# Layer norm and final norm with a token to a partition: sums, roots and reciprocals on two columns, brought back along the tokens by products with the identity

## The chip, the cores and the metric

The kernel runs on one core of a Trainium2 chip. TensorE (PE in the profile; its weight loads are PEld) multiplies matrices into PSUM; VectorE (DVE), ScalarE (ACT) and GpSimd (POOL) work on elements; SyncE (SP) issues most transfers. The metric is the device time of one execution in microseconds (us).

## The reference, cut to what matters

The program is an encoder trunk over 256 tokens with 2048 channels: a convolution module, a feed-forward layer, a gated DeltaNet, a second feed-forward layer, and a final norm. The change touches the middle of the convolution module and the final norm:

```python
u = a * jax.nn.sigmoid(gate)
u = depthwise_conv_centred(u, w_dw) + b_dw
u = jax.nn.silu(layernorm(u, ln_g, ln_b))      # mean and variance over the 2048 channels
return u @ w_pw2 + b_pw2
...
return rmsnorm(h, final_norm)                  # x * rsqrt(mean(x*x) + eps) * w
```

## The kernel before, in words

Activations lie with the channels along the 128 partitions and the 256 tokens along the free dimension, so that 2048 channels are 16 tiles of 128x256. A sum over channels is therefore a sum over partitions and over tiles. The kernel forms it on TensorE: a 128x128 matrix of ones as the stationary operand times a tile, accumulated over the tiles (line 341 in the layer norm, line 286 in the other norms). The result is a 128x256 tile whose every partition holds the same 256 sums, so the root and the reciprocal that follow run over 256 elements in each partition, and every tile can be multiplied by them at once.

Weights arrive in f32 and are split into a rounded half (`hi`, a cast on ScalarE, line 181) and the rest (`lo`, a subtraction on VectorE, line 182). A product of a weight block with an activation tile is then two or three fast matmuls. Sums of the norms are plain f32 products; in the trace each such product shows as two weight loads and two matmuls.

**The convolution loop** (`conv_module`, `for j in range(KD)`) makes one tile per turn: two 2048-deep products (lines 211 to 213), the gate, and the 31 taps of the depthwise convolution spread over TensorE (line 387), ScalarE with GpSimd (395, 396) and VectorE (404). `second(j)` then adds the tile's sum (`s1`) and, after a square on ScalarE (line 351), the sum of squares (`s2`) with `add`. The first four tiles give a rough mean (`shift`), which is taken off, so that the variance may be formed from sums.

**The layer norm** follows the last tile. In the last turn the conv chain has the priority `LAST`; five weight tiles of the next product are prepared ahead (`highs`, line 414, on ScalarE; `weights`, line 422, on VectorE). Then, in an order written out by hand for VectorE and ScalarE (`manual_schedule`): mean `dm` (465), its square `dq` (466, ScalarE), `var` (467), root `rt` (469), a small operation that loads the table of Silu (`warm`, 292), `weights(2)`, reciprocal `lr` (472), `ml` (473), and then for each tile `mul` (474), `sub` (479), Silu (480), cast (481), `low` (484). TensorE has 26 products without a use (`FILL`, line 456) after the last sum, and then the products of the next weight `pw2`, five output tiles at a time (lines 206, 207, 209).

**The final norm** (`finish`): ScalarE scales the 16 tiles of `h` (1061); the sum of squares comes as `ss` (15 tiles, summed on GpSimd) and `rest` (the last tile's square, line 275); `token_sum` (286), root (297), reciprocal `own` into PSUM (301), a copy `rstd` into SBUF by ScalarE (1067); VectorE multiplies 12 tiles by `own` (1073), GpSimd four by `rstd` (1071: tiles 1, 5, 9, 13), and each tile is stored (1074) from ScalarE's queue where its number is even, and from SP's where it is odd.

The order of the instructions in each queue is set when the program is built, by a planner that simulates the time of each instruction and takes the ready one with the highest priority; `high_priority(n)` raises it. `with tc.issue_after(x)` makes every instruction in the block that runs on the engine of `x` come behind `x` in that engine's queue; those on other engines are free. PSUM has eight banks, which the tags share: three `lin`, two `b`, one each of `sum`, `a` and `g`.

Of the kernel before, what the change touches and what calls it, by code (L numbers as in the profile page):

```python
# [26 lines left out]
PSB = {"lin": 3, "sum": 1, "a": 1, "b": 2, "g": 1}  # L27
HP = 550
OUT0 = 26
LAST = 2500  # L30
# [6 lines left out]
FIRST = 4  # L37
# [8 lines left out]
XB = 7  # L46
FIRSTS = 5
PRE = 5
FILL = 26
MORE = 2  # L50


# [25 lines left out]
def fv(ap, off, *dims):  # L78

    return bass.AP(ap.tensor, ap.offset + off, [list(ap.ap[0]), *[list(d) for d in dims]])  # L80


class Trunk:
# [199 lines left out]
    def token_sum(self, *ts):  # L283
# [2 lines left out]
            self.nc.tensor.matmul(acc, self.mat("ones"), t, start=(n == 0), stop=(n == len(ts) - 1))  # L286
        return acc

    def warm(self, func, after):

        t = self.sp.tile([P, 1], F32, tag="warm", bufs=1, name=self.nm("warm"))
        self.nc.scalar.activation(t, after[:, :1], func)
# [18 lines left out]
    def conv_module(self, next_norm):  # L311
        nc, tc, sp = self.nc, self.tc, self.sp
        self.new_h()
        self.load_first([self.pw1[0], self.pw1[KD]])
        with tc.tile_pool(name="conv", bufs=1, reuse_waits="tile") as cv:
# [6 lines left out]
            new = lambda tag, bufs: cv.tile([P, S], F32, tag=tag, bufs=bufs, name=self.nm(tag))  # L322
# [10 lines left out]
            shift = None  # L333
            sums = {}

            def add(key, t, n, last):

                if n == 0:
                    tag = "a" if key == "s1" else "sum"
                    sums[key] = self.ps.tile([P, S], F32, tag=tag, bufs=PSB[tag], name=self.nm(key))  # L340
                self.summed = nc.tensor.matmul(sums[key], self.mat("ones"), t, start=(n == 0), stop=last)

            def second(j):

                d = us[j]
                if j < SHIFTED:
                    nc.gpsimd.tensor_tensor(d, d, shift, op=ALU.subtract)
                if j >= FIRST:
                    add("s1", d, j - FIRST, j == KD - 1)
                sq = new("lsq", 2)  # L350
                self.sq_done = nc.scalar.activation(sq, d, AF.Square)
                add("s2", sq, j, j == KD - 1)
                ds.append(d)

            for j in range(KD):
# [4 lines left out]
                rstd = self.rstd  # L360
# [6 lines left out]
                with tc.high_priority(LAST if j == KD - 1 else 0):  # L367
# [6 lines left out]
                    acc = new(f"a{j}", 1)  # L374
                    npe, npool = NPE[j], NPOOL[j]
                    own = None
                    if j == KD - 1:
                        own = self.ps.tile([P, S], F32, tag="b", bufs=PSB["b"], name=self.nm("own"))
# [26 lines left out]
                    if own:  # L405
# [5 lines left out]
                        def highs(c):  # L411
                            r = raws[c][:, : CS * P]
                            hi, lo = (cv.tile([P, CS * P], F32R, tag=t, bufs=XB, name=self.nm(t)) for t in ("hi", "lo"))
                            nc.scalar.copy(hi, r)
                            pre[c] = (r, hi, lo)
                            return hi

                        def weights(c, after=None):

                            r, hi, lo = pre[c]  # L420
                            with tc.issue_after(after.ins) if after else nullcontext():
                                nc.vector.tensor_tensor(lo, r, hi.bitcast(F32), op=ALU.subtract)
                            pre[c] = [(hi[:, x * P : (x + 1) * P], lo[:, x * P : (x + 1) * P]) for x in range(CS)]

                        with tc.issue_after(scaled.ins):
                            self.warm(AF.Sqrt, tg)
                            for c in range(PRE):
                                pre_hi = highs(c)
                    if own:
# [5 lines left out]
                        t = nc.vector.tensor_tensor(acc, acc, part, op=ALU.add)  # L435
# [4 lines left out]
                            nc.vector.tensor_tensor(acc, acc, o, op=ALU.add)  # L440
                us.append(acc)
                if j < FIRST:
                    add("s1", acc, j, j == FIRST - 1)
                if j == FIRST - 1:
                    shift = new("shift", 1)
                    nc.scalar.activation(shift, sums["s1"], AF.Copy, scale=1.0 / (FIRST * P))
                    for i in range(FIRST):
                        second(i)
                elif j >= FIRST:
                    second(j)  # L450


            idle = self.ps.tile([P, 512], F32, tag="lin", bufs=PSB["lin"], name=self.nm("idle"))
            with tc.issue_after(self.summed.ins):
                for n in range(FILL):
                    nc.tensor.matmul(idle, pre_hi[:, :P], pre_hi, start=True, stop=True)

            dm, dq, var = new("dm", 1), new("dq", 1), new("var", 1)

            lr, ml = (self.ps.tile([P, S], F32, tag="b", bufs=PSB["b"], name=self.nm("ln")) for _ in range(2))  # L460
            order = range(KD)
            ys = [cv.tile([P, 2 * S], F32R, tag=f"y{j}", name=self.nm("y")) for j in order]

            with tc.high_priority(HP), tc.manual_schedule(engines={mybir.EngineType.DVE, mybir.EngineType.Activation}):
                nc.vector.tensor_scalar(dm, sums["s1"], 1.0 / D, None, op0=ALU.mult)
                nc.scalar.activation(dq, sums["s1"], AF.Square, scale=1.0 / D)
                known = nc.vector.scalar_tensor_tensor(var, sums["s2"], 1.0 / D, dq, op0=ALU.mult, op1=ALU.subtract)
                rt = self.sp.tile([P, S], F32, tag="rstd", bufs=2, name=self.nm("rstd"))
                nc.scalar.activation(rt, var, AF.Sqrt, scale=1.0, bias=self.c("eps5"))
                self.warm(AF.Silu, rt)  # L470
                weights(2)
                nc.vector.reciprocal(lr, rt)
                nc.vector.tensor_tensor(ml, dm, lr, op=ALU.mult)
                mul = lambda n: n < KD and nc.vector.tensor_tensor(ds[n], ds[n], lr, op=ALU.mult)

                def sub(n):

                    if n < KD:
                        self.begun = nc.vector.tensor_tensor(ds[n], ds[n], ml, op=ALU.subtract)
                        nc.scalar.activation(ds[n], ds[n], AF.Silu, scale=self.p("lng", n), bias=self.p("lnb", n))  # L480
                        nc.scalar.copy(ys[n][:, :S], ds[n])

                def low(n):
                    nc.vector.tensor_tensor(ys[n][:, S:], ds[n], ys[n][:, :S].bitcast(F32), op=ALU.subtract)

                mul(0)
                sub(0)
                mul(1)
                weights(3)
                sub(1)  # L490
                mul(2)
                for n in range(KD):
                    low(n)
                    if n == 1:
                        for c in range(4, PRE):
                            weights(c)
                    sub(n + 2)
                    mul(n + 3)
                    if n == 1:
                        begun = self.begun  # L500
            self.norm_begin()
            with tc.issue_after(begun.ins):
                self.ahead, self.split_ahead = [raws], pre[:PRE]
                first = self.products(self.pw2[:FIRSTS], KD, ys, wide=True, tags=("lin", "lin", "lin", "g", "a")[:FIRSTS], pool=cv, order=order)
            self.five = None
# [552 lines left out]
    def finish(self):  # L1058
        nc = self.nc
        for k in range(KD):  # L1060
            nc.scalar.activation(self.h[k], self.h[k], AF.Copy, scale=self.p("finn", k))

        own = self.ps.tile([P, S], F32, tag="b", bufs=PSB["b"], name=self.nm("own"))
        ss = [self.ss, self.rest]
        self.rsqrt(self.token_sum(*ss), 1.0 / D, self.c("eps6"), None, own)
        rstd = self.sp.tile([P, S], F32, tag="rstd", bufs=2, name=self.nm("rstd"))
        nc.scalar.copy(rstd, own)
        for k in range(KD):
            o = self.h[k]
            if k % 4 == 1:  # L1070
                nc.gpsimd.tensor_tensor(o, o, rstd, op=ALU.mult)
            else:
                nc.vector.tensor_tensor(o, o, own, op=ALU.mult)
            (nc.sync if k % 2 else nc.scalar).dma_start(self.out[:, k, :], o)
        self.free_h()
# [90 lines left out]
```

## Time and profile before

| | |
|---|---|
| runs | 2806.95, 2806.75, 2803.21 us; median 2806.75 |
| profiled execution | 2802.27 us, its span 2800.5 us |
| granted TensorE clock, mean | 0.998 |
| busy share | PE 98%, DVE 74%, ACT 63%, POOL 13% |
| convolution module up to the first product of `pw2` | 0 to 267.0 us of the span |
| last product of the program to the end | 2787.4 to 2800.5 us |

Times inside the profile count from the start of the span. A busy share is an average over stages; the two places that the change touches are two stretches of some 10 us, in which TensorE has little to do. Operations on one engine overlap at their ends, so that the start of the next can lie before the recorded end of the last.

### The profile page before, as it was taken

Reading aid. Unit: us, or ns where it says so; the run is one execution under the profiler, and the core shown is the slowest. Engines: PE = TensorE matmul, PEld = TensorE weight load, DVE = VectorE, ACT = ScalarE, POOL = GpSimd, SP = SyncE. Lnnn points to the kernel's source line nnn. Section 1 sums busy time; section 2 is a strip of 40 time slices with the busy share of each in tenths; the row PEclk is TensorE's granted clock in tenths of the full one; section 3 lists DMA queues with packets and bytes.
Section 4 is the critical chain, followed back from the end, with each engine's and each line's share of the span. In section 5 each row is a group of like instructions: output and inputs, shape, how many; then the busy total and the mean of one; then the engine's idle time right before and its main releaser. Section 6 shows DMA issues by size and latency. Waiting matters only on the chain.

```text
span 2800.5 us, 50212 instructions
## 1 busy us (share of the span) xinstructions
PE 2754.0 (98%) x18224; PEld 2510.1 (90%) x18224; DVE 2065.2 (74%) x3892; ACT 1759.7 (63%) x3716; POOL 367.9 (13%) x427
## 2 busy tenths in 40 slices
PE   8999999999999999999999999999999999999998
PEld 7998888888888889999999999998888888888887
DVE  8999876666666667889898989856666666665555
ACT  8877555555554445776978878765455555555443
POOL 3764310000000112000000000001110000000111
PEclk9999999999999999999999999999999999999999
DMA  5443565555556665776565665576666655566664
GB/s 188 137 146 127 179 202 189 189 189 190 191 188 194 198 199 176 237 235 201 174 231 168 227 197 193 182 254 189 190 209 190 191 189 188 189 189 187 189 191 139
DMA packets 170649, 532.88 MB, mean 190 GB/s; under 512 B 18944, under 2 KB 42752, under 8 KB 170400
## 3 DMA queue, kind: packets, MB, share of 16 engines
q1 hardware_dynamic: 169104, 528.37, 59.3%
q8 instruction: 143, 2.34, 0.3%
q10 hardware_dynamic: 1296, 1.30, 0.1%
q14 instruction: 106, 0.87, 0.1%
HBM read 500.69 MB, written 28.90 MB: 189 GB/s over the span
## 4 chain that ended last, share of the span: by engine, by line
PE 82%; ACT 6%; DVE 4%; DMA 4%; issue 2%; POOL 2%; SPq 0%; POOLq 0%; DVEq 0%; ACTq 0%
PE acc L207 39%; PE acc L206 20%; PE acc L213 5%; PE acc L212 5%; PE acc L211 5%; POOL a L396 2%; DVE lo L182 2%; PE psa L925 1%; PE psb L967 1%; ACT hi L181 1%; DMA raw<-in_win 1%; PE psb L990 1%; PE acc L209 1%; DMA raw<-in_wout 1%; PE psg L778 1%
## 5 line engine op out<-in xcount | busy, mean ns | idle before, releaser
L182 DVE TENSOR_TENSOR lo<-raw,hi 128x512 fp32r<-128x512 f32 x1759 | 1256.3, 718 | 641.6 <-ACT hi L181 634.3
L181 ACT CAST hi<-raw 128x512 fp32r<-128x512 f32 x1759 | 1076.3, 619 | 835.2 <-PE acc L207 658.4
L207 PE MATMUL acc<-xs,hi 128*128 128x512 f32 x2816 | 967.3, 392 | 0.0
L206 PE MATMUL acc<-xs,lo 128*128 128x256 f32 x2640 | 744.1, 282 | 0.0
L207 PEld LDWEIGHTS acc<-xs,hi 128*128 128x128 f32 x2816 | 517.0, 188 | 99.0
L211 PE MATMUL acc<-xs,hi 128*128 128x256 f32 x2064 | 585.7, 285 | 13.7 <-ACT hi L181 8.9
L213 PE MATMUL acc<-xs,lo 128*128 128x256 f32 x2064 | 586.5, 285 | 2.8 <-DVE lo L182 2.7
L212 PE MATMUL acc<-xs,hi 128*128 128x256 f32 x2064 | 585.0, 284 | 1.1 <-DVE xs L264 1.0
L206 PEld LDWEIGHTS acc<-xs,lo 128*128 128x128 f32 x2640 | 498.4, 189 | 8.4
L207 PE MATMUL acc<-hs,hi 128*128 128x512 f32 x1408 | 486.8, 391 | 0.0
L211 PEld LDWEIGHTS acc<-xs,hi 128*128 128x128 f32 x2064 | 389.6, 189 | 18.6 <-ACT hi L181 10.5
L213 PEld LDWEIGHTS acc<-xs,lo 128*128 128x128 f32 x2064 | 389.6, 189 | 11.9 <-issue 5.7
L212 PEld LDWEIGHTS acc<-xs,hi 128*128 128x128 f32 x2064 | 390.3, 189 | 6.6 <-issue 4.1
L206 PE MATMUL acc<-hs,lo 128*128 128x256 f32 x1376 | 388.3, 282 | 0.0
L207 PEld LDWEIGHTS acc<-hs,hi 128*128 128x128 f32 x1408 | 262.4, 188 | 52.8
L206 PEld LDWEIGHTS acc<-hs,lo 128*128 128x128 f32 x1376 | 260.1, 189 | 1.6
L532 POOL TENSOR_TENSOR tg<-tg,rstd 128x256 f32<-128x256 f32 x88 | 65.4, 744 | 905.6 <-ACT tg L531 905.6
L207 PE MATMUL acc<-ys,hi 128*128 128x512 f32 x512 | 177.7, 392 | 0.0
L396 POOL TENSOR_TENSOR a<-a,m 128x256 f32<-128x256 f32 x171 | 150.3, 880 | 97.3 <-ACT m L395 85.3
L206 PE MATMUL acc<-ys,lo 128*128 128x256 f32 x496 | 140.3, 284 | 2.2 <-DVE lo L182 2.2
L275 POOL TENSOR_TENSOR sq<-h 128x256 f32<-128x256 f32 x59 | 53.4, 905 | 543.4 <-DVE h L543 384.5
L711 DVE SCALAR_TENSOR_TENSOR u<-t,par_sb,u 128x254 f32<-128x254 f32 (+1 forms) x256 | 120.3, 480 | 2.3 <-ACT u L707 1.8
(239 smaller groups left out, 2910.1 us busy)
## 6 DMA issues: line engine op xcount, KB each, us to landing
raw<-in_gu SPq DMA_DIRECT2D x352, 512.0 KB, 4.5
raw<-in_win SPq DMA_DIRECT2D x194, 512.0 KB, 4.4
raw<-in_dn SPq DMA_DIRECT2D x160, 512.0 KB, 3.6
raw<-in_pw SPq DMA_DIRECT2D x94, 512.0 KB, 3.8
raw<-in_wout SPq DMA_DIRECT2D x64, 512.0 KB, 4.4
a_d<-am SPq DMA_DIRECT2D x32, 512.0 KB, 4.3
ar<-a_d SPq DMA_DIRECT2D x32, 512.0 KB, 5.0
raw<-in_dn SPq DMA_DIRECT2D x32, 256.0 KB, 3.6
```

What stands on the lines that cost most here:

```text
L181: nc.scalar.copy(hi, r)
L182: nc.vector.tensor_tensor(lo, r, hi.bitcast(F32), op=ALU.subtract)
L206: nc.tensor.matmul(acc[:, S:], lo, a[:, :S], start=False, stop=False)
L207: nc.tensor.matmul(acc, hi, a, start=first, stop=last)
L209: nc.tensor.matmul(acc[:, S:], lo, a[:, :S], start=False, stop=False)
L211: nc.tensor.matmul(acc[:, :S], hi, a[:, :S], start=first, stop=False)
L212: nc.tensor.matmul(acc[:, :S], hi, a[:, S:], start=False, stop=False)
L213: nc.tensor.matmul(acc[:, :S], lo, a[:, :S], start=False, stop=last)
L275: (nc.vector if last else nc.gpsimd).tensor_tensor(sq, h, h, op=ALU.mult)
L396: nc.gpsimd.tensor_tensor(acc, acc, m, op=ALU.add)
L532: nc.gpsimd.tensor_tensor(tg, tg, rstd, op=ALU.mult)
L711: nc.vector.scalar_tensor_tensor(u[:, lo:hi], t[:, lo + s : hi + s], w(i), u[:, lo:hi], op0=ALU.mult, op1=ALU.add)
```

## The change: what it does

The tile becomes the stationary operand, and a narrow constant the moving one. `sums["all"]` is one PSUM tile of 128x4: for each tile and each half `b` of the tokens, the 128x128 block of the tile is loaded as weights and multiplied by four columns of `sel`, of which one is all ones and three are zero. So the sums of 128 tokens land in one column, a token to a partition: columns 0 and 1 hold `s1`, 2 and 3 hold `s2`. The sums of the first four tiles, which give `shift`, stay as they were.

`dm`, `dq`, `var`, `rt`, `rc` and `mc` are then 128x2. `dq` moves from ScalarE to VectorE. `along` brings a column back: the column, read 128 times with a step of 0, is the stationary operand, the identity the moving one, and the product is a 128x128 block whose every partition holds the column's 128 values along the tokens. Two such products write `lr`, two write `ml`, both in PSUM as before. The 26 products without use become 6 behind the last sum and 10 behind `ml`.

Three orders change. The last tile's square gets the priority `LAST`. The products of `pw2` and the casts of their weights also stand behind that square (`issue_after(self.sq_done.ins)`). `weights(2)` comes after the reciprocal and `mc`.

In the final norm the squares' tiles are the stationary operand too, with one column of ones; each half of the tokens has its PSUM bank, its root (128x1) on ScalarE; one reciprocal of 128x2 follows. `along` is called twice: into `own`, which VectorE reads, and into `other`, which ScalarE copies to `rstd` for GpSimd.

```diff
-FILL = 26
+FILL = (6, 10)
...
+    def along(self, out, col):
+        for b in range(2):
+            t = self.nc.tensor.matmul(out[:, b * P : (b + 1) * P], fv(col, b, (0, P)), self.mat("ident"), start=True, stop=True)
+        return t
...
+                for b in range(2):
+                    self.summed = nc.tensor.matmul(sums["all"], t[:, b * P : (b + 1) * P], self.c("sel", 4 * (2 * key + b), 4),
+                                                   start=(n == 0 and b == 0), stop=(last and b == 1))
...
-                self.sq_done = nc.scalar.activation(sq, d, AF.Square)
-                add("s2", sq, j, j == KD - 1)
+                with tc.high_priority(LAST if j == KD - 1 else 0):
+                    self.sq_done = nc.scalar.activation(sq, d, AF.Square)
+                add(1, sq, j, j == KD - 1)
...
-                nc.vector.tensor_scalar(dm, sums["s1"], 1.0 / D, None, op0=ALU.mult)
-                nc.scalar.activation(dq, sums["s1"], AF.Square, scale=1.0 / D)
-                known = nc.vector.scalar_tensor_tensor(var, sums["s2"], 1.0 / D, dq, op0=ALU.mult, op1=ALU.subtract)
-                rt = self.sp.tile([P, S], F32, tag="rstd", bufs=2, name=self.nm("rstd"))
+                nc.vector.tensor_scalar(dm, s1, 1.0 / D, None, op0=ALU.mult)
+                nc.vector.tensor_tensor(dq, dm, dm, op=ALU.mult)
+                nc.vector.scalar_tensor_tensor(var, s2, 1.0 / D, dq, op0=ALU.mult, op1=ALU.subtract)
                 nc.scalar.activation(rt, var, AF.Sqrt, scale=1.0, bias=self.c("eps5"))
                 self.warm(AF.Silu, rt)
+                nc.vector.reciprocal(rc, rt)
+                nc.vector.tensor_tensor(mc, dm, rc, op=ALU.mult)
                 weights(2)
-                nc.vector.reciprocal(lr, rt)
-                nc.vector.tensor_tensor(ml, dm, lr, op=ALU.mult)
+                idles(FILL[0], self.summed)
+                self.along(lr, rc)
+                idles(FILL[1], self.along(ml, mc))
...
-            with tc.issue_after(begun.ins):
+            with tc.issue_after(begun.ins), tc.issue_after(self.sq_done.ins):
...
-        own = self.ps.tile([P, S], F32, tag="b", bufs=PSB["b"], name=self.nm("own"))
-        ss = [self.ss, self.rest]
-        self.rsqrt(self.token_sum(*ss), 1.0 / D, self.c("eps6"), None, own)
+        rt, rc = (self.sp.tile([P, 2], F32, tag=f"tail{n}", bufs=1, name=self.nm("rt")) for n in range(2))
+        sums = [self.ps.tile([P, 1], F32, tag=t, bufs=PSB[t], name=self.nm("tsum")) for t in ("sum", "a")]
+        for n, t in enumerate((self.ss, self.rest)):
+            for b in range(2):
+                nc.tensor.matmul(sums[b], t[:, b * P : (b + 1) * P], self.mat("ones")[:, :1], start=(n == 0), stop=(n == 1))
+        for b in range(2):
+            nc.scalar.activation(rt[:, b : b + 1], sums[b], AF.Sqrt, scale=1.0 / D, bias=self.c("eps6"))
+        nc.vector.reciprocal(rc, rt)
+
+        own, other = (self.ps.tile([P, S], F32, tag="b", bufs=PSB["b"], name=self.nm("own")) for _ in range(2))
+        self.along(own, rc)
+        self.along(other, rc)
         rstd = self.sp.tile([P, S], F32, tag="rstd", bufs=2, name=self.nm("rstd"))
-        nc.scalar.copy(rstd, own)
+        nc.scalar.copy(rstd, other)
```

More of the change, by code (lines that the diff above doesn't have):

```diff
@@ L336, in add @@
             def add(key, t, n, last):
[L338 to L341, printed above, removed]
+                if key == "first":
+                    if n == 0:
+                        sums[key] = self.ps.tile([P, S], F32, tag="a", bufs=PSB["a"], name=self.nm(key))
+                    nc.tensor.matmul(sums[key], self.mat("ones"), t, start=(n == 0), stop=last)
+                    return
+                if "all" not in sums:
+                    sums["all"] = self.ps.tile([P, 4], F32, tag="sum", bufs=PSB["sum"], name=self.nm("s"))
+                for b in range(2):
+                    self.summed = nc.tensor.matmul(sums["all"], t[:, b * P : (b + 1) * P], self.c("sel", 4 * (2 * key + b), 4),
+                                                   start=(n == 0 and b == 0), stop=(last and b == 1))
             def second(j):
@@ L348, in second @@
                 if j >= FIRST:
-                    add("s1", d, j - FIRST, j == KD - 1)
+                    add(0, d, j, False)
                 sq = new("lsq", 2)
-                self.sq_done = nc.scalar.activation(sq, d, AF.Square)
-                add("s2", sq, j, j == KD - 1)
+                with tc.high_priority(LAST if j == KD - 1 else 0):
+                    self.sq_done = nc.scalar.activation(sq, d, AF.Square)
+                add(1, sq, j, j == KD - 1)
                 ds.append(d)
@@ L442, in conv_module @@
                 if j < FIRST:
-                    add("s1", acc, j, j == FIRST - 1)
+                    add("first", acc, j, j == FIRST - 1)
                 if j == FIRST - 1:
                     shift = new("shift", 1)
-                    nc.scalar.activation(shift, sums["s1"], AF.Copy, scale=1.0 / (FIRST * P))
+                    nc.scalar.activation(shift, sums["first"], AF.Copy, scale=1.0 / (FIRST * P))
                     for i in range(FIRST):
@@ L453, in conv_module, with idles @@
             idle = self.ps.tile([P, 512], F32, tag="lin", bufs=PSB["lin"], name=self.nm("idle"))
[L454 to L458, printed above, removed]
+            def idles(n, after):
+                with tc.issue_after(after.ins):
+                    for _ in range(n):
+                        nc.tensor.matmul(idle, pre_hi[:, :P], pre_hi, start=True, stop=True)
+            dm, dq, var, rt, rc, mc = (cv.tile([P, 2], F32, name=self.nm("col")) for _ in range(6))
+            s1, s2 = sums["all"][:, :2], sums["all"][:, 2:]
             lr, ml = (self.ps.tile([P, S], F32, tag="b", bufs=PSB["b"], name=self.nm("ln")) for _ in range(2))
```

## Prediction

> **What bounds the kernel now.** I read the page's busy shares first, then the chain of waits around the layer norm and at the end, then timelines of single engines there, and the convolution loop by windows. The whole is bound by TensorE:
>
> ```profile
> PE 2754.0 (98%) x18224; PEld 2510.1 (90%) x18224; DVE 2065.2 (74%) x3892; ACT 1759.7 (63%) x3716; POOL 367.9 (13%) x427
> ```
>
> Time won elsewhere counts only where TensorE waits. It waits in the layer norm; in the chain of waits (start, length, what) the last 8 us before its first product at 267.00 are mostly other engines' work:
>
> ```profile
> 258.79 1.04 ACT hi L181 x2
> 259.82 0.33 ACT lsq L351
> ...
> 261.01 0.42 DVE var L467
> 261.44 0.60 DVE lo L422
> 262.04 1.75 DVE ln L472
> 263.81 0.43 DVE ln L473
> ...
> 267.00 0.50 PE acc L207
> ```
>
> Two weight casts stand ahead of the last square (line 351); a reciprocal over 256 elements takes 1.75; `lo` L422 (0.60) and `ml` (L473, 0.43) lie on the chain too. The other place is the end, all engines in order of time:
>
> ```profile
> 2788.86 0.51 ACT L1061 ACTIVATE h<-h,par_sb 128x256 f32<-128x256 f32 x1 [6.37 <-DVE sq L275]
> 2788.88 0.70 PE L286 MATMUL tsum<-sq,cst_sb 128*128 128x256 f32 x2 [1.50 <-DVE sq L275]
> 2789.62 0.47 ACT L297 ACTIVATE rstd<-tsum,cst_sb 128x256 f32<-128x256 f32 x1 [0.25 <-PE tsum L286]
> 2790.13 1.76 DVE L301 RECIPROCAL own<-rstd 128x256 f32<-128x256 f32 x1 [1.30 <-ACT rstd L297]
> 2791.92 0.37 ACT L1067 COPY rstd<-own 128x256 f32<-128x256 f32 x1 [1.83 <-DVE own L301]
> 2792.32 4.07 DVE L1073 TENSOR_TENSOR h<-h,own 128x256 f32<-128x256 f32 x12 [0.44 <-ACT rstd L1067]
> 2792.37 2.77 POOL L1071 TENSOR_TENSOR h<-h,rstd 128x256 f32<-128x256 f32 x4 [17.90 <-ACT rstd L1067]
> ```
>
> From the square to the first multiplication it is 3.5 us, half of it the reciprocal.
>
> **The convolution loop: the sums themselves.** Tiles 4 to 15 add `s1`, all 16 add `s2`: 28 sums, each one f32 product of 256 columns before (two matmul records) and two of 4 columns after (four records). In the loop TensorE is nearly full (columns: window, length, PE, PEld, DVE, ACT, POOL, clock, DMA share, GB/s):
>
> ```profile
> 135.00:150.00 15.00, 14.32 (x112) 13.80 (x112) 14.67 (x28) 11.67 (x28) 9.42 (x11) 1.00 0.43 141
> 47.00:240.00 193.00, 190.68 (x1446) 183.64 (x1445) 183.06 (x353) 155.74 (x365) 136.22 (x153) 1.00 0.45 145
> ```
>
> It idles 193 - 190.68 = 2.3 us in the whole loop, so a dearer sum would be paid nearly in full. Rows for the price, stretches of such records in order of time: the sums as they are, f32 products with 128x128 weights and 32 columns, and with 4 rows and 4 columns:
>
> ```profile
> 163.00 0.59 PE L341 MATMUL s<-a,cst_sb 128*128 128x256 f32 x2
> 1135.43 0.53 PE L680 MATMUL psb<-v,cst_sb 128*128 128x32 f32 x4
> 1136.02 0.61 PE L680 MATMUL psb<-v,cst_sb 128*128 128x32 f32 x4
> 1196.42 0.28 PE L747 MATMUL pssum<-cst_sb,rs 4*128 4x4 f32 x2
> ```
>
> and the length of one record (mean ns, the figure behind the comma):
>
> ```profile
> L680 PE MATMUL psb<-v,cst_sb 128*128 128x32 f32 x8 | 1.1, 265 | 0.0
> L747 PE MATMUL pssum<-cst_sb,rs 4*128 4x4 f32 x16 | 2.3, 209 | 0.0
> L341 PE MATMUL s<-lsq,cst_sb 128*128 128x256 f32 x32 | 9.3, 383 | 1.1 <-ACT lsq L351 1.1
> ```
>
> A record after the first costs 0.59 - 0.38 = 0.21 us in the sum of now, so a pair 0.43. Among the products of 32 columns it is (0.61 - 0.27) / 3 = 0.11, so four cost 0.44. That is no difference, and I take 0: columns fall from 256 to 4, but each new record loads new weights, and with few columns nothing covers the load. Bounds: by line 747, (0.28 - 0.21) rounds to 0.08, four cost 0.32, and 28 sums win 3.1 us (it loads only 4 rows, so it is the farther row); upwards, if leaving the group costs one more load of 0.11, 28 x (0.11 + 0.01) = 3.4 us are lost, of which TensorE's 2.3 idle us may take part: I set 2.5. The Trainium skill agrees with the 0.11: "TensorE: Matmul & The Clock Gate", section LDWEIGHTS, makes a load of 128 columns 107 ns whatever the rows; its section on the back-to-back issue gap would have a product of up to 64 columns cost some 25 ns, which is a rival below.
>
> **The layer norm.** What stands around the chain, engine by engine:
>
> ```profile
> 256.10 2.68 ACT L414 CAST hi<-raw 128x512 fp32r<-128x512 f32 x5
> 258.69 1.13 ACT L181 CAST hi<-raw 128x512 fp32r<-128x512 f32 x2
> 262.00 1.28 ACT L292 ACT_TABLE_LOAD   x1
> 265.05 0.60 ACT L480 ACTIVATE a<-a,par_sb 128x256 f32<-128x256 f32 x1 [1.56 <-DVE a L479]
> 257.88 0.42 DVE L435 TENSOR_TENSOR a<-a,part 128x256 f32<-128x256 f32 x1
> 264.15 0.41 DVE L474 TENSOR_TENSOR a<-a,ln 128x256 f32<-128x256 f32 x1
> 260.54 6.27 PE L456 MATMUL idle<-hi 128*128 128x512 f32 x26
> ```
>
> Prices of small operations:
>
> ```profile
> L750 DVE TENSOR_SCALAR rt<-pssum 128x8 f32<-128x8 f32 x3 | 0.5, 165 | 0.0
> L292 ACT ACTIVATE warm<-rstd 128x1 f32<-128x1 f32 x1 | 0.2, 203 | 0.0
> ```
>
> Step by step. The tile is complete at 258.30. ScalarE is free of line 414's issues at 258.69, where line 181 starts now; the square goes there instead: 258.69 to 259.10 (1.04 us earlier, the first term). The sum of squares: four records from 259.16, three steps of 0.11, the last record's 0.27 and some 0.05 for the first load: about 259.82. `s1` and `s2` share one PSUM tile, and its last writer is this sum, so `dm` can no longer run ahead: three dependent VectorE operations of 0.17 and 0.03 of handing over each, done 260.45. Root 0.20: 260.70. Reciprocal and `mc` at 0.17 to 0.25 each (no row has a short reciprocal; 1.76 for 256 elements is 7 ns an element, so nearly all is fixed cost): `rc` 260.93, `mc` 261.13. TensorE meanwhile has six idle products at 6.27 / 26 = 0.24: from 259.7 to 261.1. So `along(lr)` starts about 261.05, when both are ready: four records, done by 261.7, `ml` by 262.15. `weights(2)` fills VectorE until 261.7. First `mul` about 261.75 against 264.15: **2.4 us earlier**. From `mul` to the first product all is as now, 267.00 - 264.15 = 2.85, so the product starts at 264.6; the ten idle products end at 262.0 + 2.4 = 264.4, just ahead.
>
> What else must be early: the table of Silu, loaded behind the root: 260.70 + 1.28 + 0.20 = 262.2; the first Silu is due 262.65. That reserve of 0.45 is what is late next. The two casts of line 181 now start at 259.1 and end at 260.2, ahead of a root that is due at 260.5; they cost nothing, and 0.5 at most if one more stood there. `dq` leaves ScalarE at no price, being in the sum above. Bounds: -2.7 (reciprocal at 0.17, no idle product in the way) and -1.0 (the square stays behind the casts, and 0.4 of the rest is lost to the table).
>
> The start moves all that follows by this. The next weights' transfers are released by casts that move too, and the DMA queues are empty there; TensorE is the bound behind, so the gain is kept.
>
> **The end.** `ss` is multiplied early, as now. From the square's end, just before 2788.86: the scaling of line 1061 holds ScalarE to 2789.33; the first half's sum is there at 2789.3, the second's at 2789.5, two roots of 0.20 end at 2789.8, reciprocal 2790.0, `along(own)` 2790.05 to 2790.75, first multiplication on VectorE 2790.8 instead of 2792.32: 1.5 us. But `other` comes 0.44 later, 2791.2, its copy of 0.37 ends 2791.6, and GpSimd starts at 2791.65 instead of 2792.37: 0.7 us. Which of them sets the end is told by the stores:
>
> ```profile
> L1074 ACTq DMA_DIRECT2D out<-h x8: 338/358/470, 2792.8 to 2796.7; - x8
> L1074 SPq DMA_DIRECT2D out<-h x8: 333/406/416, 2793.1 to 2797.0; - x8
> ```
>
> SP's eight issues run from 2793.1, when GpSimd's first tile is done (2792.37 + 0.72), to 2797.0, some 0.55 apart, and the last one comes 0.6 behind the end of VectorE's work (2792.32 + 4.07). ScalarE's begin 2792.8. So the end follows SP, SP's first issue follows GpSimd: **0.7 us**. Bounds: -1.5, if the end follows VectorE, and +0.2, if TensorE's clock is halved by then: the four records of each `along` take 0.9 more together, against 0.7. The clock does fall in this stretch of now, 2 us behind the last product:
>
> ```profile
> 2790.00:2791.60 1.60, 0.00 (x0) 0.00 (x0) 1.47 (x1) 0.09 (x1) 0.00 (x0) 1.00 0.00 0
> 2791.70:2795.00 3.30, 0.00 (x0) 0.00 (x0) 2.86 (x10) 0.37 (x1) 2.63 (x4) 0.50 0.44 154
> ```
>
> **Sum.** -2.4 - 0.7 + 0 = -3.1 us, with the bounds together -7.3 (2.7 + 1.5 + 3.1) to +1.7 (2.5 + 0.2 - 1.0). The profiled execution took 2802.27, so a like one would take 2799.2. The runs shown lie at 2803.21, 2806.75 and 2806.95; the four average 2804.8, the median lies 4.5 above the profiled one. I set the forecast from the average: 2804.8 - 3.1 = **2801.7**.
>
> **Rivals.** (B) The weight loads of the narrow sums are covered after all, and each record costs what line 680's second did in the first group, where 0.53 is 0.08 less than the second group's 0.61: 0.11 - 0.08 = 0.03. Then a sum costs 4 x 0.03 = 0.12 instead of 0.43, 28 sums win 8.7, and the time is 2804.8 - 3.1 - 8.7 = 2793.0. The 25 ns of the Trainium skill's section on the issue gap, named above, say nearly this. Against it: only one record in each stretch behind a wide product is so cheap. Chance 0.08. (C) Slower: the planner lays the loop out anew, since its sums are other instructions, and the new order costs stalls. The stall is there: 15.00 - 14.32 = 0.68 us in the 15 us from 135 on, 2.3 in the 193 us from 47 to 240. If each of the 13 stretches of 15 us in these had it, 13 x 0.68 - 2.3 = 6.5 are lost, and 6.5 - 3.1 = +3.4: 2808.2. It decides from 3.1 us of new stalls. For it: VectorE is busy 183.06 of the 193 us, so order matters; against it: the priorities in the loop are unchanged. Chance 0.15. (D) The layer norm's gain is given back before the feed-forward layer, as VectorE and ScalarE, not TensorE, pace the `pw2` products; only the end's 0.7 stays: 2804.1. For it: ScalarE and VectorE stand in the chain there (from 287.46 on); against it: they begin earlier too, with 2 us less of VectorE's work. Chance 0.15. The forecast has 0.62.
>
> **How the numbers follow.** 0.2% is 5.6 us, about what a measurement can tell here. Faster by more: all of B and 0.12 of the forecast's, toward its bound: 0.20. Slower by more: the worse half of C: 0.07. Within: 0.73. The range for 8 in 10 is 2797 (just under 5 below the forecast, leaving out B) to 2808 (C's price, and the upper runs).
>
> **What would show it.** Right: square at the issue that line 181's first cast has now; first `mul` some 3.4 us behind the tile's last addition (5.85 now); the new sums' records 0.11 apart; SP's first store 0.7 earlier, VectorE's first multiplication 1.5. Wrong: the root waiting on casts, Silu on its table, `along` on idle products or at clock 0.50; loop turns longer or shorter by more than 0.2 us.

## The result: 0.8% slower, where 0.1% faster was forecast

The changed kernel takes 2826.27 us (median of 4 runs, 2824.06 to 2831.71); the kernel before took 2806.85 us in the same comparison. The ratio is 1.0079, with a 95% interval of 1.0063 to 1.0095: slower by 18 to 27 us. The forecast was 2801.7, its range ended at 2808.

The profiled execution took 2825.0 us, its span 2823.2 us against 2800.5. Four instructions that both kernels have, each the first of its kind in its stage, tell where the difference arose. Timeline rows of the kernel after (start, length, engine, line; before each "..." a stage lies):

```profile
265.02 0.50 PE L207 MATMUL acc<-y,hi 128*128 128x512 f32 x1
...
1110.92 0.41 DVE L671 TENSOR_TENSOR t<-acc,rstd 128x256 f32<-128x256 f32 x1
...
1925.84 0.48 DVE L264 SCALAR_TENSOR_TENSOR xs<-h,par_sb,xs 128x256 fp32r<-128x256 f32 x1
...
2811.90 0.43 DVE L275 TENSOR_TENSOR sq<-h 128x256 f32<-128x256 f32 x1
```

and of the kernel before (its first `pw2` product, 267.00, stands in the prediction):

```profile
1106.99 0.41 DVE L652 TENSOR_TENSOR t<-acc,rstd 128x256 f32<-128x256 f32 x1
...
1907.94 0.72 DVE L264 SCALAR_TENSOR_TENSOR xs<-h,par_sb,xs 128x256 fp32r<-128x256 f32 x1
...
2788.40 0.42 DVE L275 TENSOR_TENSOR sq<-h 128x256 f32<-128x256 f32 x1
```

| stage | after - before at its end | change in the stage |
|---|---|---|
| convolution and layer norm, to the first `pw2` product | -1.98 | -1.98 |
| `pw2`, first feed-forward layer, to the first gate of the DeltaNet | +3.93 | +5.91 |
| DeltaNet and its output product, to the norm behind it | +17.90 | +13.97 |
| second feed-forward layer, to the last square | +23.50 | +5.60 |
| the final norm, to the end of the span | +22.7 | -0.8 |

Both places that the change edits became shorter. All of the loss lies in three stages whose products the change does not touch (of `pw2` it only sets what they stand behind in the queues). TensorE stays the bound there; it is busy longer:

```profile
PE 2781.9 (99%) x18290; PEld 2520.3 (89%) x18290; DVE 2059.8 (73%) x3893; ACT 1762.3 (62%) x3716; POOL 366.5 (13%) x427
```

**The feed-forward layers.** The same window, 400 to 1000 us, lies wholly inside the first layer in both kernels. The weight loads in it, by windows (columns: window, length, PEld busy and count, clock, DMA share, GB/s), first before, then after:

```profile
400.00:1000.00 600.00, 530.41 (x3453) 1.00 0.61 191
```

```profile
400.00:1000.00 600.00, 523.01 (x3430) 1.00 0.61 190
```

3453 products fit into 600 us before and 3430 after, 0.67% fewer, at clock 1.00 in both and with TensorE busy all the 600.00 us. A timeline of TensorE shows the single product; before:

```profile
500.03 0.28 PE L206 MATMUL acc<-xs,lo 128*128 128x256 f32 x1
500.15 0.40 PE L207 MATMUL acc<-xs,hi 128*128 128x512 f32 x1
...
503.85 0.28 PE L206 MATMUL acc<-xs,lo 128*128 128x256 f32 x1
```

and after:

```profile
499.94 0.28 PE L206 MATMUL acc<-xs,lo 128*128 128x256 f32 x1
500.06 0.39 PE L207 MATMUL acc<-xs,hi 128*128 128x512 f32 x1
...
503.44 0.28 PE L206 MATMUL acc<-xs,lo 128*128 128x256 f32 x1
```

Before, eleven pairs take 503.85 - 500.03 = 3.82 us, 347 ns each; after, ten take 3.50, 350 ns each. The recorded length of a product does not tell it: 0.39 in both. It shows in the distance from start to start.

**The DeltaNet.** Its instructions are the same, but in the built program 919 of VectorE's 2477 positions there hold another instruction than before, and ScalarE's and SyncE's order differs too: the planner laid the stage out anew.

### The profile page after: what moved, and what is told of

It reads as the page before. It is cut to its first block, busy times and chain, and to the rows that moved or that the text cites. A ratio compares the mean times of both kernels' runs of the same rounds, so it can differ in the third digit from the quotient of the medians.

```text
span 2823.2 us, 50343 instructions
## 1 busy us (share of the span) xinstructions
PE 2781.9 (99%) x18290; PEld 2520.3 (89%) x18290; DVE 2059.8 (73%) x3893; ACT 1762.3 (62%) x3716; POOL 366.5 (13%) x427
## 4 chain that ended last, share of the span: by engine, by line
PE 88%; DVE 4%; ACT 4%; DMA 3%; issue 2%; POOL 0%; SPq 0%; POOLq 0%; ACTq 0%; DVEq 0%
PE acc L207 40%; PE acc L206 19%; PE acc L213 7%; PE acc L212 7%; PE acc L211 7%; PE psa L944 1%; DVE lo L182 1%; PE psb L1009 1%; PE psb L986 1%; PE acc L209 1%; PE r L400 1%; ACT hi L181 1%; PE psg L797 1%; DMA y<-y_d 1%; DMA raw<-in_pw 1%
```

## Experiments

Two suspects could reach stages that nobody edited. The *addresses*: the final norm's two new tiles (`tail0`, `tail1`, 32 bytes a partition each) stand in a pool that is laid out ahead of the activations, so that `xs`, `h`, `hs` and `ys` lie 64 bytes further in every partition; the split weights (`hi`, `lo`) did not move. In the kernel before, the activation tiles begin at a multiple of 256 bytes (`xs[0]` at 56576), `hi` and `lo` 224 bytes behind one (35040, 43232). And the *order* of the DeltaNet.

### Addresses alone: the kernel before with its tiles moved

One tile that is used for nothing but a table load is made longer, which moves everything behind it and leaves every instruction and the order as they are:

```diff
-        t = self.sp.tile([P, 1], F32, tag="warm", bufs=1, name=self.nm("warm"))
+        t = self.sp.tile([P, N], F32, tag="warm", bufs=1, name=self.nm("warm"))[:, :1]
```

N = 24 moves the activations by 64 bytes, 16 by 32, 72 by 256.

> The kernel before with nothing changed but the one-column scratch tile of warm made 24 columns wide (96 bytes instead of 32; one column is used), so that activations, residual and all stage tiles start 64 bytes later, as in the changed kernel. Theory A: slower by 22 to 28 us (the changed kernel lost 19.4 and had won some 2 to 4), about 2832; starts 232 ns apart in the feed-forward stage, and 120 in the convolution loop where 117 were. Rivals B and C: no difference, 2807.

> The kernel before with the scratch tile of warm 16 columns wide, so that all behind it starts 32 bytes later. Theory A as a boundary of 64 bytes (each row read costs a further piece if it starts inside one): slower by about the same or more than a shift of 64, over 20 us. Theory A as a question of 64-byte halves of 128 alone (operand starts in the upper half): about 0. Rivals B and C: 0.

> The kernel before with the scratch tile of warm 72 columns wide: all behind it starts 256 bytes later, and every moving operand keeps its place within 256 bytes. Theory A (the start of the moving operand within 256 bytes, with the stationary one left as it is, sets the distance of matmul starts): 228 and 118 ns in the feed-forward stage as in the kernel before, and the time within 3 us of it. Rival B' (any move away from the kernel before costs some 0.3 to 0.6%, for a reason of its own, as all four moves tried so far did): 2815 to 2823.

Measured: 64 bytes 2819.50 us, ratio 1.0053 [1.0037, 1.0070]; 32 bytes 2822.22, 1.0065 [1.0046, 1.0084]; 256 bytes 2802.89, 0.9994 [0.9985, 1.0003]. The windows of the first feed-forward layer, for 64 bytes:

```profile
400.00:1000.00 600.00, 523.24 (x3430) 1.00 0.60 190
```

for 32 bytes:

```profile
400.00:1000.00 600.00, 522.99 (x3406) 1.00 0.59 188
```

and for 256 bytes:

```profile
400.00:1000.00 600.00, 529.71 (x3453) 1.00 0.60 191
```

The 64 bytes give the very count of the changed kernel, 3430; 256 bytes give that of the kernel before. TensorE reads nothing else that moved in this window, so the pace of a product depends on where its moving operand begins, and the change of address alone costs half a per cent. The sizes were forecast too high: 64 bytes cost 14.6 us by the medians, not 22 to 28, and 32 bytes 17.4, not over 20.

The other operand was moved too: the parameters' tile ahead of the weights was made 32 bytes longer, so that `hi` and `lo` begin at a multiple of 256, with the activations 128 (N = 32) or 256 bytes (N = 64) further.

```diff
-        self.par = self.cp.tile([P, NRES], F32, name="par_sb")
+        self.par = self.cp.tile([P, NRES + 8], F32, name="par_sb")
...
-        nc.scalar.dma_start(self.par, self.par_d[:, :NRES])
+        nc.scalar.dma_start(self.par[:, :NRES], self.par_d[:, :NRES])
```

> The kernel before with 32 bytes more behind the parameters and the scratch tile of warm 128 bytes wide: the split weights (stationary operands), which start 96 bytes off a multiple of 128 in both kernels, start on a multiple of 128; the activations move by 128 and keep theirs. If the start of the stationary operand counts as the moving one's does: faster, by up to 20 us (4 ns in each of some 18000 loads that are not covered). If only the moving operand counts: within 3 us of the kernel before.

> The kernel before with the split weights moved to a multiple of 128 (by 32 bytes) and everything behind the small tiles moved by 256, so that against the shift by 256 only the weights differ. If the weights' start made the kernel with both at a multiple of 128 slow: 206 to 207 some 120 ns instead of 118, and 8 to 15 us slower than the kernel before. If it was the 128 bytes of the activations: as the kernel before.

Measured: 2822.55 us, ratio 1.0063 [1.0048, 1.0079], 3420 loads in the window; and 2824.14 in a single run, 3408 loads. With the activations in their good place the weights' new start costs 45 of 3453 loads. Neither forecast for the first of these kernels came true: it is slower, by 18 us; the second, forecast at 8 to 15 us more or none, takes 20 more. Of the two weight addresses tried, the round one is the worse, 224 bytes behind a multiple of 256 the better. Which pairs of starts are good in general was not mapped.

### Addresses taken out of the change

First by making the two tail tiles 64 bytes each, so that all moves by 128:

```diff
-        rt, rc = (self.sp.tile([P, 2], F32, tag=f"tail{n}", bufs=1, name=self.nm("rt")) for n in range(2))
+        rt, rc = (self.sp.tile([P, 16], F32, tag=f"tail{n}", bufs=1, name=self.nm("rt"))[:, :2] for n in range(2))
```

> The changed kernel, whole, with its two small tiles of the final norm 64 bytes a partition each instead of 32, so that everything allocated behind them starts 128 bytes later than in the kernel before instead of 64. Theory A (the two tiles moved the operands of the matmuls by 64 bytes, and a matmul whose moving operand starts 64 bytes off a multiple of 128 takes some 3.5 ns longer): matmul starts in the feed-forward stage 228 and 118 ns apart again, and 2 to 6 us under the kernel before, about 2803. Rival B (the new instructions themselves, or the order that the planner made of them, slow the later stages): as slow as the changed kernel, 2826. Rival C (lower clock after the layer norm): 2826 too.

Then by putting them into buffers that exist, so that nothing moves behind the convolution module (inside it the tiles `y` do):

```diff
-        rt, rc = (self.sp.tile([P, 2], F32, tag=f"tail{n}", bufs=1, name=self.nm("rt")) for n in range(2))
+        rt, rc = (self.sp.tile([P, 2], F32, tag=t, bufs=2, name=self.nm("rt")) for t in ("ss", "rstd"))
```

> The changed kernel, whole, with the two small tiles of the final norm put into slots that the kernel has anyway (the free one of ss, one of rstd), so that no address of activations, residual or stage tiles differs from the kernel before; the tiles y of the convolution module start on a multiple of 128 where they were 64 off. Theory A: 228 and 118 ns in the feed-forward stage, and 2 to 4 us under the kernel before (layer norm 1.0 and final norm 0.8, read from the changed kernel's profile, and up to 1 of the pw2 products). Rival B (the new code slows the later stages): slower by 15 us or more.

Measured: 2814.15 us, ratio 1.0035 [1.0021, 1.0049], and 2811.13 us, 1.0025 [1.0015, 1.0036]. Both forecasts, a gain of 2 to 6 and of 2 to 4 us, failed, and so did their rivals, a loss of 19 us and of 15 or more. The window has 3452 loads in both. The same instructions as above, with nothing moved:

```profile
264.02 0.50 PE L207 MATMUL acc<-y,hi 128*128 128x512 f32 x1
...
1104.44 0.41 DVE L671 TENSOR_TENSOR t<-acc,rstd 128x256 f32<-128x256 f32 x1
...
1919.30 0.48 DVE L264 SCALAR_TENSOR_TENSOR xs<-h,par_sb,xs 128x256 fp32r<-128x256 f32 x1
...
2799.50 0.42 DVE L275 TENSOR_TENSOR sq<-h 128x256 f32<-128x256 f32 x1
```

Against the kernel before: -2.98, -2.55, +11.36, +11.10. The feed-forward layers keep what they get to within 0.5 us; the 5.91 and 5.60 are gone, so they were the addresses. The DeltaNet still loses 13.9 us. Both kernels have the new order there. What the addresses cost in the DeltaNet is not settled: against the kernel before, the profile with 64 bytes takes 4.1 us more in it, that with 32 bytes 0.9 less, with the order of before in both.

### The layer norm with its clock

Of the layer norm's forecast gain only a part was there (below); TensorE's clock was halved in it. Five more products without use, behind the last tap's product, were to keep TensorE at work while the sums are awaited:

```diff
+                with tc.issue_after(tapped.ins):
+                    for _ in range(5):
+                        nc.tensor.matmul(idle, xs[0][:, :P], xs[0], start=True, stop=True)
```

> As the changed kernel at the old addresses, and five more products without use (on activations that are there) behind the last tap product of the last tile, in the 1.3 us in which TensorE waits for the tile. If the halved clock that the layer norm had in the changed kernel from 259.4 on comes from TensorE's near-idle stretch there, it does not come here: the idle products and the products with the identity take 0.23 and 0.11 us each instead of twice that, and the first pw2 product starts 0.8 to 1.2 us sooner than without. If the clock falls whatever stands there, no difference.

Measured: 2810.55 us, 1.0028 [1.0017, 1.0038], no different from the kernel without them. Its layer norm, TensorE and VectorE in order of time:

```profile
261.25 1.05 PE L292 MATMUL ln<-cst_sb,col 128*128 128x128 f32 x8
...
264.82 0.50 PE L207 MATMUL acc<-y,hi 128*128 128x512 f32 x1 [0.22 <-DVE y L506]
```

```profile
257.88 0.42 DVE L447 TENSOR_TENSOR part<-r,part 128x256 f32<-128x256 f32 x1 [1.48 <-PE r L400]
258.40 0.43 DVE L448 TENSOR_TENSOR a<-a,part 128x256 f32<-128x256 f32 x1
```

From the last tile (258.83) to the first product it is now 5.99 us, against 8.70 before: 2.7 us less, where the forecast had 2.4. But this execution has its halved stretch from 252.0 to 255.4, where it delays the taps of the last tile, and VectorE waits 1.48 us for them. The stage as a whole gains 2.18 (264.82), less than the 2.98 above. So the profile prices the new chain at full clock; that the five products kept the clock up is not shown, as they run from 257.84 on, behind the halved stretch.

### The order of the DeltaNet

The planner's order changes with the number of products without use ahead of `along`. With 17 in place of 6 the order is that of the kernel before; with 16, 752 of VectorE's positions differ. Apart from that one product nothing else differs between the two, and no address moves.

```diff
-FILL = (6, 10)
+FILL = (17, 10)
```

> The changed kernel with no address moved (the two small tiles of the final norm in buffers that exist), as in e6, and 17 idle products in place of 6 ahead of the products that bring the reciprocals back. In the built program VectorE's, ScalarE's and SyncE's work in the linear attention then stands in the order of the kernel before; with 6 idle products 919 of VectorE's 2477 positions there differ. Theory (what e6 lost between 1100 and 1900 us, about 14 us, is the order that the planner chose): no loss there, within 2 us; ahead of it e6's gain of 3.7 us less at most 11 x 0.24 = 2.6 us for the added idle products, so 1.1 to 3.7; with 0.8 us at the end the kernel takes 2 to 4 us less than before, ratio 0.9985 to 0.9995. Rival (the changed code or its earlier start slows the linear attention by itself): the 14 us stay, ratio 1.003 to 1.005.

> As e9, with one idle product less (16), which is 0.24 us of work; the planner's order of the linear attention then differs from before's in 752 of VectorE's 2477 positions. Theory (order): the linear attention between 1100 and 1900 us takes some us more or less than in e9, by the size of e6's loss between 4 and 15 us more, though nothing else differs; the kernel 4 to 15 us above e9. Rival (the order costs nothing): within 1 us of e9.

Measured: 17 products 2806.68 us, ratio 1.0009 [1.0000, 1.0018]; 16 products 2811.04, 1.0025 [1.0017, 1.0034]. One product without use less, 0.24 us of work, makes the kernel 4.1 us slower in the mean (11 runs each; 95% interval of their ratio 1.0008 to 1.0021, by resampling the runs). That is what the forecast for 16 said, and so the order has a price. But the forecast for 17, a gain of 2 to 4 us, failed as well as its rival's loss: it lands between. Its part on the DeltaNet, no loss within 2 us, did not come true in the profile either. The first gate and the norm behind the DeltaNet, with 17 products:

```profile
1107.95 0.41 DVE L671 TENSOR_TENSOR t<-acc,rstd 128x256 f32<-128x256 f32 x1
...
1918.68 0.73 DVE L264 SCALAR_TENSOR_TENSOR xs<-h,par_sb,xs 128x256 fp32r<-128x256 f32 x1
```

and with 16:

```profile
1104.42 0.41 DVE L671 TENSOR_TENSOR t<-acc,rstd 128x256 f32<-128x256 f32 x1
...
1915.85 0.61 DVE L264 SCALAR_TENSOR_TENSOR xs<-h,par_sb,xs 128x256 fp32r<-128x256 f32 x1
```

The DeltaNet takes 9.8 us more than before with 17 products and 10.5 with 16. The profiled execution with 17 was the longest of its 11 runs (2812.04 us), so these two profiles do not show where the 4.1 us lie; only the runs tell the two kernels apart.

A part of the price is seen in the clock. Here is what TensorE had in two neighbouring stretches of the DeltaNet, by windows (PE, PEld, DVE, ACT, POOL, clock, DMA share, GB/s), in the kernel with 6 products and nothing moved:

```profile
1880.00:1883.40 3.40, 1.24 (x7) 0.84 (x7) 1.74 (x5) 2.05 (x6) 0.00 (x0) 1.00 0.95 293
1883.40:1890.20 6.80, 5.86 (x24) 5.18 (x23) 2.53 (x6) 2.66 (x7) 0.00 (x0) 0.50 0.69 252
```

and in the kernel before:

```profile
1880.00:1883.40 3.40, 3.40 (x29) 3.27 (x29) 1.45 (x3) 0.95 (x4) 0.00 (x0) 1.00 0.90 272
1883.40:1890.20 6.80, 6.80 (x41) 6.00 (x41) 3.67 (x9) 5.72 (x19) 1.63 (x1) 1.00 0.39 150
```

In the new order TensorE has only 1.24 us of work in the 3.40 us ahead of the halved stretch; in the old one it is busy throughout at that time of the span, though not at quite the same point of the work. Halved stretches last 3.41 us or a multiple, and each 3.41 us take 1.7 us of TensorE's work. The profiled executions have, counted in lengths of 3.41 us between 1107 and 1908 us: before none, before's order with 17 products two, 16 products three, 6 products six, the changed kernel three. One profile each does not tell the orders apart by this count: the kernel before with moved weights and activations 128 bytes further has three too. The mean granted clock over all runs is 0.9964 before, 0.9966 with 17 products, 0.9956 with 16, 0.9946 with 6, and over all runs here 0.001 of clock goes with 1.87 us (one fitted slope, with a level for each kernel). Between 16 and 17 products this is 1.9 of the 4.1 us. Between 6 and 17, which differ in 11 products without use too, it is 2 x 1.87 = 3.7 of the 4.5 us between their medians. So about half of the order's price in the cleaner pair goes with the clock; that the order makes it fall more often was not tested by itself.

"TensorE: Matmul & The Clock Gate" of the Trainium skill, Part 1, has the clock set in free-running windows of 3413 ns, at other places in each run; the stretches here agree in length, and they lie at other places in each profile. It ties the half rate to an idle TensorE in the window before; the first row above agrees in direction, with 1.24 of 3.40 us busy. How little work brings the clock down is not measured here.

### What is left with before's order

With 17 products one address was still off: the ring of two buffers for `rstd` stood one buffer further. The root of the layer norm was put back into it:

```diff
-            dm, dq, var, rt, rc, mc = (cv.tile([P, 2], F32, name=self.nm("col")) for _ in range(6))
+            dm, dq, var, rc, mc = (cv.tile([P, 2], F32, name=self.nm("col")) for _ in range(5))
+            rt = self.sp.tile([P, 2], F32, tag="rstd", bufs=2, name=self.nm("rstd"))
```

> As e9, with the root of the layer norm in the ring of two buffers where the root of the kernel before stood; in e9 that ring turns by one buffer, so that every later norm's factor (rstd) lies 1024 bytes off its place before. With it, the addresses and the order of everything behind the layer norm are those of the kernel before, up to the final norm. Rival (the turned ring, or what else of address or order e9 left, costs what e9 still lacks): the linear attention as before, ratio 0.9985 to 0.9995. Theory (the ring doesn't matter; what e9 lacks is the 11 added idle products, half-clock stretches and small transfers in the linear attention that do not come earlier with the work before them): as e9, 2804 to 2809, ratio 1.000 to 1.002, and in the trace ScalarE's wait for the copied decays (cb out of c_d) near 1143 us is over 1.5 us where it is 0.66 in the kernel before.

Measured: 2807.00 us, 1.0013 [1.0004, 1.0022], as the theory had it and as with the ring turned; the ring shows no effect. This profile has no halved stretch in the DeltaNet:

```profile
266.36 0.50 PE L207 MATMUL acc<-y,hi 128*128 128x512 f32 x1 [0.24 <-DVE y L504]
...
1106.12 0.41 DVE L672 TENSOR_TENSOR t<-acc,rstd 128x256 f32<-128x256 f32 x1
...
1912.42 0.73 DVE L264 SCALAR_TENSOR_TENSOR xs<-h,par_sb,xs 128x256 fp32r<-128x256 f32 x1
...
2793.11 0.42 DVE L275 TENSOR_TENSOR sq<-h 128x256 f32<-128x256 f32 x1
```

-0.64, -0.87, +4.48, +4.71: with order and addresses of the kernel before, the DeltaNet still takes 5.35 us more. It loses them in two places: 2.7 between 1141 and 1165 us, and 4.2 behind 1830 (VectorE's operations compared one by one; between them it wins 1.5). In both, ScalarE waits for transfers. The waits from 1135 to 1170 us (engine, line, waited for: sum, times, longest), before:

```profile
ACT hi L181 <- DMA raw<-in_win: 1.1, 1, 1.1
...
ACT e L794 <- DMA cb<-c_d: 0.7, 1, 0.7
```

and with 17 products and the ring put back:

```profile
ACT hi L181 <- DMA raw<-in_win: 4.5, 2, 3.2
...
ACT e L814 <- DMA cb<-c_d: 2.4, 1, 2.4
```

The decays `cb`, which go out to memory (`c_d`) and come back as copies for all partitions, are awaited for 2.4 us, where the kernel before waited 0.7. That wait is over 2 us in all five kernels with the new layer norm in which `xs` has its old place (2.05 to 2.76), and 0.95 in the one below that has the old layer norm. It does not come with the new layer norm as such: where `xs` lies 128 bytes further it is 1.1, and in the changed kernel 1.3 in two waits. Behind 1830 us the picture is mixed: from 1830 to 1895, ScalarE's wait for `y` out of memory grows from 10.3 to 12.6 us, that for weights falls from 4.9 to 1.4, and what holds the stage there was not found. So more is lost at the first place than the 0.87 that had been won ahead of it: the work leaves it 1.8 us later than in the kernel before, after longer waits for transfers. Why, when order, addresses and amounts are the same, stays open.

### The final norm alone

The kernel before with the new final norm, in buffers that exist; order and addresses as before.

> The kernel before with the final norm of the change alone (narrow sums, roots and reciprocals of two columns, brought back twice by products with the identity), in buffers that exist, so that no address moves; layer norm as before, and the order of the linear attention is that of before. Theory: nothing changes ahead of the end, and the end is 0.7 to 0.8 us shorter: 2803.5 to 2806 beside before's 2804.5 to 2806.8, ratio 0.9995 to 0.9999, which this measurement can hardly tell from 1. Rival (the end of the changed kernel gains only because it starts late): the end as long as before, ratio 1.000.

Measured: 2803.98 us, ratio 1.0000 [0.9991, 1.0009]. The gain is too small for the runs, but the profile shows it:

```profile
2789.80 0.42 DVE L275 TENSOR_TENSOR sq<-h 128x256 f32<-128x256 f32 x1
...
2792.18 4.06 DVE L1088 TENSOR_TENSOR h<-h,own 128x256 f32<-128x256 f32 x12 [0.80 <-PE own L292]
2793.08 2.77 POOL L1086 TENSOR_TENSOR h<-h,rstd 128x256 f32<-128x256 f32 x4 [17.22 <-ACT rstd L1082]
```

From the square's start to the end of the span (2800.5) 10.7 us, against 12.1 before: 1.4 less, between the forecast 0.7 and its bound of 1.5. No version that was run beats the kernel before by more than the measurement can tell.

## Why the prediction was wrong, step by step

**The convolution loop: right.** The forecast was 0 within -3.1 and +2.5. The last tile is complete at 257.27, 1.0 us earlier than before. TensorE is busy 192.79 of the 193 us from 47 on, where it was 190.68, so the narrow sums are not cheaper. VectorE in order of time:

```profile
256.85 0.42 DVE L448 TENSOR_TENSOR a<-a,part 128x256 f32<-128x256 f32 x1
...
258.77 0.16 DVE L482 TENSOR_SCALAR col<-s 128x2 f32<-128x2 f32 x1 [0.29 <-PE s L352]
258.97 0.16 DVE L483 TENSOR_TENSOR col<-col 128x2 f32<-128x2 f32 x1
259.16 0.16 DVE L484 SCALAR_TENSOR_TENSOR col<-s,col 128x2 f32<-128x2 f32 x1
259.69 0.17 DVE L487 RECIPROCAL col<-col 128x2 f32<-128x2 f32 x1 [0.36 <-ACT col L485]
...
261.76 0.42 DVE L493 TENSOR_TENSOR a<-a,ln 128x256 f32<-128x256 f32 x1 [1.11 <-PE ln L292]
```

Rival B, 8.7 us from covered loads, is out.

**The layer norm: the steps right, -0.95 in place of -2.4 in this pair of profiles, for the clock.** From tile to first product it is 265.02 - 257.27 = 7.75 us against 8.70. The square went ahead of the casts (257.66), the three small operations took 0.2 each from start to start, the reciprocal 0.17. What the sum left out is the clock: "`along(lr)` ... four records" and the six idle products at 0.24 were both priced at full clock. The chain of waits of the kernel after has them at half:

```profile
258.13 0.61 PE s L352 x4
258.73 2.13 PE idle L471 x6
260.86 1.71 PE ln L292 x8
262.57 2.42 PE idle L471 x10
```

Six idle products take 2.13 for 1.4 and the eight records of `along` 1.71 for 1.05 (their length above, at full clock). The clock from 259.4 to 263.4 is 0.58 in the mean. The prediction named "`along` at clock 0.50" as a sign against it, but gave it a price only at the end. The profile of before, with which it is compared, has the stage at full clock. At half clock the old layer norm is longer too, and its chain also runs over TensorE; here in the kernel with the final norm alone, whose clock is at half from 259.9 to 263.3:

```profile
259.71 7.52 PE idle L462 x26
```

From tile to first product that one takes 9.95 us, and the old layer norm 9.8 to 10.0 in all four profiles with the halved stretch there. The new one with six products takes 7.6 to 7.9 in three. So at like clocks the change gains some 2.2 us at half and 2.7 at full, the latter with the five products more: the term of 2.4 was about right, and the -0.95 sets a halved stage against a full one. The halved stretch falls into the stage in four of seven profiles with the old layer norm and in six of seven with the new.

**The end: 0.8 in place of 0.7, right by another route.** VectorE's first multiplication comes 2.4 us behind the square's start instead of 3.9, as forecast, but GpSimd's first only 0.3 sooner (3.68 against 3.97), because the copy for it had come behind the first store in ScalarE's queue:

```profile
2814.74 0.35 ACTq L1102 DMA_DIRECT2D out<-h  x1
2815.13 0.37 ACT L1095 COPY rstd<-own 128x256 f32<-128x256 f32 x1 [1.85 <-DVE h L1101]
```

In three later kernels with this end (16 products, 17 with the ring put back, the final norm alone) the copy stands ahead of the store, GpSimd starts 3.28 behind the square, and the end gains 1.4. But with 6 products and nothing moved the copy again stands behind the store and the end still gains 1.2, so the copy does not explain all of the difference.

**"TensorE is the bound behind, so the gain is kept": this step failed, and it decides.** It took for granted that a stage with untouched code takes the same time from wherever it starts. It holds for the feed-forward layers, once no address moves (within 0.5 us over 840 us in the two profiles shown). But the prediction gave no price to where the two new tiles of the final norm put everything else: 5.91 + 5.60 = 11.5 us of the 23.5. And it let the planner lay out anew only the convolution loop (rival C, +6.5 there): the kind was right and the place wrong. The loop lost nothing, the DeltaNet 850 us later lost 14, of which 5 to 10 are still there in the two profiles with the order of before. In rival D the gain was to be given back ahead of the feed-forward layer; with 6 products and nothing moved 0.4 us of it are, up to the DeltaNet, and it is the DeltaNet that takes more than was won.

**How the loss divides.** By the medians: taking the addresses out brings the ratio from 1.0079 to 1.0025, some 15 us; restoring the order brings it to 1.0009 or 1.0013, some 4, though it costs 11 idle products more; the rest, 2.5 to 3.6 us, is what the DeltaNet and the idle products take beyond what layer norm and end give. The first step is shown by moving the addresses alone (1.0053 for 64 bytes, 15 us), the second by the pair of 16 and 17; the third is read from two profiles and not tested alone, and its cause stays open.

## What to carry to other kernels

A new tile, however small, can move the operands of every matmul behind it: compare the start addresses of the built program before and after an edit, and put small tiles where nothing lies behind them. Where a planner orders the queues by simulated time, an edit can reorder a stage far away; compare the orders too, before a loss there is put down to the edit itself. And a chain of small steps that runs over TensorE inherits its clock, so it should be priced at full and at half, and two profiles of such a stage compared at like clocks.

## What the runs showed of the hardware

- The start of an f32r product's moving operand, together with that of its weights, sets its pace. In 600 us of the same products at clock 1.00: 3453 loads at a multiple of 256 bytes, 3452 at 128 beyond one, 3430 at 64, 3406 at 32. With the weights 32 bytes further, at a multiple of 256, it is 3408 to 3420. The Trainium skill, "SBUF — State Buffer", section Operand start alignment, asks for a multiple of the element's size and says that this is about what is allowed, not about speed; here the speed differs by up to 1.4% among starts that are all allowed.
- The recorded length of such a product (0.39) does not show this; only the distance from start to start, or the count in a window, does.
- TensorE's clock fell to half for 3.41 us at a time or a multiple, at other places in each profile; ahead of the stretch at 1883.4 TensorE had been busy for 1.24 of 3.40 us.
- A reciprocal of 128x2 takes 0.17 us on VectorE, of 128x256 1.76; a root of 128x2 on ScalarE took 0.29.
